# A second layer in another order of tokens, with half rounds in the value products

## The chip, the cores and the metric

The kernel runs on one core of a Trainium2 chip. The metric is the device time of one execution in microseconds (us), and lower is better.

## What is computed

Two layers of a small transformer on 256 tokens of width 2048, with 256 context tokens beside them, batch 1. The first layer is a Fourier mixer, the second an attention with 64 query heads of 64 columns on 8 key-value heads. Each layer ends in a projection (`w_out`) that is added to its input through a gate; the output is the normed `x`. What bears on the change is the attention:

```python
q, k, v, z = jnp.split(h @ w_in, [D_BRANCH, D_BRANCH + kvw, D_BRANCH + 2 * kvw], axis=-1)
kc, vc = jnp.split(hc @ w_in[:, D_BRANCH:D_BRANCH + 2 * kvw], 2, axis=-1)
q = _axial_rope(q...); k = _axial_rope(k...)
valid = abs(qpos - kpos) <= 128            # token against token; the context is seen by all
p = softmax(concat([where(mask, q @ keys * 64 ** -0.5, -1e30), sink]))[..., :-1]
y = (p @ vals) * silu(z)
x = x + gate * (y @ w_out)
return _rmsnorm(x, final_g)
```

A query in one half of the 256 tokens sees a key in the other half only if they are at most 128 apart. Counted in natural blocks of 32 tokens, a query block and a key block more than 4 blocks apart have no pair that the mask lets through.

## The kernel before

Everything is float32. Weights and activations are split into a high and a low part (`split`, `half_split`: a ScalarE cast and a VectorE difference), and a product is three matmuls (`mm3`, lines 79 to 81). Weights come in 1 MB loads on SP's queue (`raw`, L47).

**Order of tokens.** The host lays tokens out in an order of its own, `_perm`: tokens 0 to 128, then 255 down to 129. It suits the Fourier layer, and the kernel before keeps it to the end. The tiles have two blocks of 128 tokens, `tb` = 0 and 1, so that block 1 holds token 128 in its row 0 and then 255, 254 and so on. `rope` and `mask` (loaded by `cload`, L57, on POOL's queue, and followed there by `sink`) are tables in that order. The host puts the output back in order.

**Start of the second layer.** For each of 16 k-tiles, VectorE scales x (L931), ScalarE adds the shift and rounds to the high part `h` (L932), VectorE forms the low part (L933); s = 0 is the tokens, s = 1 the context. The k/v projection follows; `v` is copied out of PSUM by ScalarE (L959) and written to a DRAM tensor `vd` by POOL's queue (L961). `nsink` (L907) is a VectorE operation on `sink`. This part is ordered by the framework's planner, from its estimates of durations; the loop over heads is ordered by hand.

**The loop over heads.** 64 steps i, 8 for each key-value head: scores (`s_mm`), the mask and the maximum in one VectorE operation (L1215), exponentials and normalisation on ScalarE, and a VectorE transpose by blocks of 32 (`x_turn`, L1245) into `pall`, whose partitions are four groups g of 32 queries' blocks and whose columns are (head pair k, block of queries t, row i). Between them stand units of the projections (`emit_unit`). Queries are turned by `q_turn` (L1048).

**Value products.** After each 8 steps, `stage_o` (L1252), in two halves with a unit between, multiplies `vrep` and `pall`: for each key block b (16 of them: 4 + 4 blocks of tokens, 8 of context), each hh of 2 and each g of 4 one matmul of 32 rows by 64 columns with 256 moving columns. The 8 matmuls of one b lie in 8 different tiles of TensorE's array; all 16 b add up in PSUM. I call the 8 matmuls of one b a round. `emit_y` (L1261) multiplies the result by 0.5 and by z.

**The end.** `w_out` is applied to column blocks; `x2` holds the layer's input, loaded from the DRAM tensor `x1d` by POOL's queue (L1338). `finish(tb, ...)` takes the norm's root, scales four tiles of [128 tokens, 512 columns], in the order c = 2, 0, 3, 1, and stores each by one DMA to `out` (L1407): on SP's queue, and for tb = 1, c = 1 on ScalarE's. The stores of tb = 1 are the last thing that the kernel does.

Of the kernel before, what the change touches and what calls it, by code (L numbers as in the profile page):

```python
# [16 lines left out]
P = 128  # L17
# [12 lines left out]
def tile_dit(ctx: ExitStack, tc: tile.TileContext, a: dict, out: bass.AP):  # L30
# [24 lines left out]
    def cload(name, shape, q=None, pool=const):  # L55
        t = pool.tile(shape, F32, tag=name, name=name)
        (q or nc.gpsimd).dma_start(t, a[name])  # L57
        return t
# [841 lines left out]
    lay0.close()  # L900

    l1c = ctx.enter_context(tc.tile_pool(name="l1c", reuse_waits="tile", bufs=1))
    rope = cload("rope", [P, 2, 2, 64], pool=l1c)
    mask = cload("mask", [P, 2, 512], pool=l1c)
    sink = cload("sink", [P, 64], pool=l1c)
    nsink = l1c.tile([P, 64], F32, name="nsink")
    V.tensor_scalar(nsink, sink, -1.0, None, op0=ALU.mult)  # L907
# [12 lines left out]
    with tc.tile_pool(name="h1", reuse_waits="tile", bufs=16) as h1p:  # L920
        hx1 = []
        kT = []
        with tc.tile_pool(name="kvp", reuse_waits="tile", bufs=2) as kvp:
            hc1 = []
            for k in range(KT):
                hx = h1p.tile([P, 512], F32R, tag="h1", name="h1")
                hc = kvp.tile([P, 512], F32R, tag="h1c", name="h1c", bufs=16)
                t = kvp.tile([P, 512], F32, tag="ht", name="ht")
                for s, h in ((0, hx), (1, hc)):
                    q = slice(s * N, (s + 1) * N)  # L930
                    V.scalar_tensor_tensor(t[:, q], x1[k][:, q], gs1[:, k, s : s + 1], r_bc1[:, q] if k else rows1[s], op0=ALU.mult, op1=ALU.mult)  # L931
                    hx_act = S.activation(h[:, 0:N], t[:, q], AF.Identity, bias=sh1[:, k, s : s + 1]).ins  # L932
                    hx_end = V.scalar_tensor_tensor(h[:, N : 2 * N], t[:, q], sh1[:, k, s : s + 1], h[:, 0:N].bitcast(F32), op0=ALU.add, op1=ALU.subtract).ins  # L933
                if k == 0:
                    hx_first = (hx_end, hx_act)
                    with tc.issue_after(hx_act):
                        while turned:
                            x1_out(*turned.pop(0), kvp)
                hx1.append(hx)
                hc1.append(hc)  # L940
            o = [[psum() for _ in range(2)] for _ in range(4)]
            for kg in range(8):
                w = [(kv_h, kv_l)] if kg == 0 else ws_split(raw(a["wkv"][kg]))
                for j in range(2):
                    k = kg * 2 + j
                    if k == 1:
                        with tc.issue_after(hx_first[0]), tc.issue_after(hx_first[1]):
                            w.append(half_split(kv_raw, 1))
                    wh, wl = w[j]
                    for tb in range(4):  # L950
                        h = (hx1, hc1)[tb // 2][k]
                        c = (tb % 2) * P
                        for kv in range(2):
                            q = slice(kv * 512, (kv + 1) * 512)
                            mm3(o[tb][kv], h[:, c : c + P], h[:, N + c : N + c + P], wh[:, q], wl[:, q], k == 0, k == KT - 1)
            kr = []
            for tb in range(4):
                t = kvp.tile([P, 512], F32, tag="v", name="v", bufs=4)
                S.copy(t, o[tb][1])  # L959
                for g in range(4):  # L960
                    nc.gpsimd.dma_start(vd[:, :, tb * 4 + g, :].rearrange("h j d -> j h d"), t[g * 32 : g * 32 + 32].rearrange("p (h d) -> p h d", d=64))  # L961
                t = kvp.tile([P, 512], F32, tag="kr", name="kr", bufs=4)
                if tb < 2:
                    roped(t, o[tb][0], tb, kvp)
                else:
                    S.copy(t, o[tb][0])
                kr.append(t)
            for hp in range(4):
                o = psum()
                for tb in range(4):  # L970
                    PE.transpose(o[:, tb * P : (tb + 1) * P], kr[tb][:, hp * P : (hp + 1) * P], ident)
                t = act()
                S.copy(t, o)
                kT.append(t)
# [5 lines left out]
        with tc.tile_pool(name="ye", reuse_waits="tile", bufs=6) as yep, ExitStack() as ats:  # L980
# [62 lines left out]
            def q_turn(p2, qr):  # L1043
                o = psum()
                for pr in range(2):
                    for tb in range(2):
                        c = (p2 * 2 + pr) * P
                        PE.transpose(o[:, (pr * 2 + tb) * P : (pr * 2 + tb + 1) * P], qr[tb][:, c : c + P], ident)  # L1048
                return o

            def q_cast(hk, p2, o):
# [192 lines left out]
            def x_turn(i):  # L1244
                V.transpose(pall[:, i % 2, :, i // 2 % 4].rearrange("p b t i -> p t b i"), pts.pop(i).rearrange("p t (b j) -> p t b j", j=32))  # L1245

            def stage_o(oo, half):
                for b in range(half * 8, half * 8 + 8):
                    for hh in range(2):
                        for g in range(4):  # L1250
                            q = slice(g * 32, g * 32 + 32)
                            PE.matmul(oo[g][hh * 64 : hh * 64 + 64, 0:N], vrep[0][q, b, :], pall[q, hh, b].rearrange("p k t i -> p (k t i)"), start=b == 0, stop=b == 15)  # L1252

            def emit_y(hk, oo):
                th = szs.pop(hk)
                for p2 in range(2):
                    y1.append(act())
                    for g in range(4):
                        dst, z = (x.rearrange("p k (t g i) -> p k t g i", t=2, g=4)[:, :, :, g, :] for x in (y1[-1].rearrange("p (k n) -> p k n", k=2), th[:, p2 * 2 : p2 * 2 + 2]))
                        src = oo[g][:, p2 * P : (p2 + 1) * P].rearrange("p (k t i) -> p k t i", k=2, t=2)  # L1260
                        V.scalar_tensor_tensor(dst, src, 0.5, z, op0=ALU.mult, op1=ALU.mult)  # L1261

            for i in range(10):
                w_prep(pos[0])
# [65 lines left out]
            with tc.tile_pool(name="fin", reuse_waits="tile", bufs=1) as fp:  # L1330
# [4 lines left out]
                for tb in range(2):  # L1335
                    x2.append([act() for _ in range(4)])
                    for c in range(4):
                        nc.gpsimd.dma_start(x2[tb][c], x1d[tb, :, c * 512 : (c + 1) * 512])  # L1338
                fg = fp.tile([P, D], F32, name="fg")
                nc.gpsimd.dma_start(fg, a["fg"].broadcast_to([P, D]))  # L1340
                ss = fp.tile([P, P], F32, name="ss")
# [54 lines left out]
                def finish(tb, col, base):  # L1396
                    r, v, t = (fp.tile([P, 1], F32, name=f"f{n}{tb}") for n in "rvt")
                    root(r, v, t, ss[:, col : col + 1], base)
                    for c in (2, 0, 3, 1):
                        t = x2[tb][c]  # L1400
                        if c == 3:
                            V.scalar_tensor_tensor(t, t, r, fg[:, c * 512 : (c + 1) * 512], op0=ALU.mult, op1=ALU.mult)
                        elif c == 2:
                            V.tensor_scalar(t, t, r, None, op0=ALU.mult)
                        else:
                            S.activation(t, t, AF.Copy, scale=r)
                        (nc.scalar if tb and c == 1 else nc.sync).dma_start(out[tb * P : (tb + 1) * P, c * 512 : (c + 1) * 512], t)  # L1407

                held = []
                for kg in range(8):  # L1410
# [139 lines left out]
```

## Time and profile before

| | before |
|---|---|
| median of 3 runs | 1770.1 us (1769.8 to 1770.34) |
| profiled execution, device time | 1769.88 us |
| its span | 1768.1 us |
| TensorE (PE) busy | 1754.8 us, 99% |
| VectorE (DVE) busy | 1377.2 us, 78% |
| ScalarE (ACT) busy | 878.1 us, 50% |
| POOL busy | 184.5 us, 10% |
| value products, L1252 | 2048 records, 60.3 us, from 1190.8 to 1619.9 us |
| last stores, L1407 with tb = 1 | issued from 1762.6 us on |

The span runs from the first to the last instruction of the profiled execution; the device time has 1.8 us around it. PE is TensorE's matmuls, PEld its weight loads; SPq, ACTq and POOLq are the queues that issue DMAs. A row of a group reads: line, engine, operation, output and input by the program's names, shapes, count; then busy time in us and mean ns of one; then idle time just before it and what ended it. A row of the timeline reads: start and length in us, engine, line, operation, count, and in brackets the idle time before. A row of a line's instructions has durations as ns min/median/max, then first and last start. In the DMA view the first line is the mean busy share of the 16 DMA engines in 40 slices of the stretch, in tenths, and the second what they moved.

### The profile page before, as it was taken

To read this page: it belongs to the slowest core of one execution; us is meant where nothing else is said; L and a number is where in the kernel's file an instruction comes from. 1 tells how busy PE (TensorE), PEld (TensorE's weight loads), DVE (VectorE), ACT (ScalarE), POOL (GpSimd) and SP (SyncE) were. 2 spreads that over 40 slices of the span, in tenths; PEclk is the share of its full clock that TensorE was granted. 3 is DMA by queue.
4 is the path that set the end of the run, shared out by engine and by line. 5 is a ranking of instruction groups with operands and counts; after the bars stand their busy time and mean duration, and the time that the engine had idled before them with its cause. 6 is when DMAs were issued, how large, how long until landed. Compare 5 with 4: busy or idle time off the path is not lost.

```text
span 1768.1 us, 28034 instructions
## 1 busy us (share of the span) xinstructions
PE 1754.8 (99%) x10967; PEld 1480.5 (84%) x10967; DVE 1377.2 (78%) x2318; ACT 878.1 (50%) x1522; POOL 184.5 (10%) x223
## 2 busy tenths in 40 slices
PE   9999999999999999999999999999999999999998
PEld 7669999998888888888888888888888888887886
DVE  6769999978897887587986473798889888987455
ACT  6545444543222232333332352687778777876343
POOL 0001000020000010000000001133123302301000
PEclk9999999999999999999999999999999999999999
DMA  9994655476766777654566333544444444446553
GB/s 389 422 381 167 210 206 207 167 274 226 304 255 247 262 275 266 259 208 156 207 240 236 113 142 108 188 146 156 155 153 147 139 148 156 146 159 235 197 183 141
DMA packets 69108, 370.20 MB, mean 209 GB/s; under 512 B 8816, under 2 KB 11008, under 8 KB 35440
## 3 DMA queue, kind: packets, MB, share of 16 engines
q1 hardware_dynamic: 55600, 328.63, 50.5%
q0 software_dynamic: 9488, 32.95, 5.5%
q10 hardware_dynamic: 3888, 6.83, 1.1%
q8 instruction: 86, 1.41, 0.3%
q14 instruction: 46, 0.38, 0.1%
HBM read 353.16 MB, written 15.21 MB: 208 GB/s over the span
## 4 chain that ended last, share of the span: by engine, by line
PE 97%; ACT 1%; DVE 1%; DMA 0%; issue 0%; SPq 0%; DVEq 0%; ACTq 0%
PE ps L79 26%; PE ps L81 26%; PE ps L80 26%; PE ps L1177 7%; PE ps L1175 3%; PE ps L1252 3%; PE ps L347 2%; PE ps L1207 2%; PE ps L1206 2%; PE ps L1048 0%; DMA xn<-in_x 0%; PE ps L662 0%; PE ps L628 0%; PE ps L363 0%; DVE wl L1125 0%
## 5 line engine op out<-in xcount | busy, mean ns | idle before, releaser
L69 ACT CAST wh<-raw 128x1024 fp32r<-128x1024 f32 x178 | 186.9, 1053 | 402.9 <-PE ps L80 345.2
L70 DVE TENSOR_TENSOR wl<-raw,wh 128x1024 fp32r<-128x1024 f32 x178 | 219.8, 1235 | 137.9 <-ACT wh L69 137.8
L80 PE MATMUL ps<-hx,wh 128*128 128x512 f32 x700 | 272.6, 389 | 0.0
L79 PE MATMUL ps<-hx,wh 128*128 128x512 f32 x700 | 271.1, 390 | 0.0
L81 PE MATMUL ps<-hx,wl 128*128 128x512 f32 x700 | 271.1, 390 | 0.0
L1125 DVE TENSOR_TENSOR wl<-raw,wh 128x1024 fp32r<-128x1024 f32 x142 | 191.2, 1352 | 56.5 <-ACT wh L1119 56.0
L1119 ACT CAST wh<-raw 128x1024 fp32r<-128x1024 f32 x142 | 148.8, 1048 | 70.9 <-PE ps L80 58.2
L699 DVE CUSTOM_DVE_ANT_0 raw<-raw,cb 128x1024 f32<-128x1024 f32 x128 | 155.0, 1220 | 35.5 <-DMA raw<-in_adw 34.7
L79 PEld LDWEIGHTS ps<-hx,wh 128*128 128x128 f32 x700 | 131.4, 188 | 27.9 <-ACT hx L432 0.8
L81 PEld LDWEIGHTS ps<-hx,wl 128*128 128x128 f32 x700 | 131.5, 188 | 27.2
L80 PEld LDWEIGHTS ps<-hx,wh 128*128 128x128 f32 x700 | 131.5, 188 | 27.2
L699 DVE CUSTOM_DVE_ANT_0 junk<-raw,cb 128x1024 f32<-128x1024 f32 x96 | 117.2, 1221 | 27.4 <-DMA raw<-in_adw 14.1
L1177 PE MATMUL ps<-h,wh 128*128 128x512 f32 x512 | 127.3, 391 | 0.0
L79 PE MATMUL ps<-wh,h 128*128 128x512 f32 x320 | 124.9, 397 | 0.2 <-ACT h L932 0.2
L80 PE MATMUL ps<-wl,h 128*128 128x512 f32 x320 | 124.9, 390 | 0.0
L81 PE MATMUL ps<-wh,h 128*128 128x512 f32 x320 | 124.6, 391 | 0.0
L1224 ACT ACTIVATE p<-ps,mx 128x512 f32<-128x512 f32 x128 | 86.8, 683 | 52.9 <-DVE mx L1215 52.8
L1177 PEld LDWEIGHTS ps<-h,wh 128*128 128x128 f32 x512 | 94.2, 188 | 18.1
L1215 DVE CUSTOM_DVE_ANT_0 ps<-ps,mask,nsink 128x512 f32<-128x512 f32 x128 | 91.1, 752 | 0.5
L80 PE MATMUL ps<-act,wh 128*128 128x512 f32 x234 | 91.0, 389 | 0.0
L81 PE MATMUL ps<-act,wl 128*128 128x512 f32 x234 | 90.3, 390 | 0.3 <-DVE wl L70 0.3
L79 PE MATMUL ps<-act,wh 128*128 128x512 f32 x234 | 89.7, 389 | 0.0
(362 smaller groups left out, 3959.8 us busy)
## 6 DMA issues: line engine op xcount, KB each, us to landing
raw<-in_adw SPq DMA_DIRECT2D x64, 1024.0 KB, 4.9
raw<-in_wz SPq DMA_DIRECT2D x58, 1024.0 KB, 4.8
raw<-in_awp SPq DMA_DIRECT2D x32, 1024.0 KB, 12.4
raw<-in_wo SPq DMA_DIRECT2D x32, 1024.0 KB, 4.8
raw<-in_wq SPq DMA_DIRECT2D x32, 1024.0 KB, 4.7
raw<-in_wu SPq DMA_DIRECT2D x25, 1016.0 KB, 5.0
raw<-in_wo1b SPq DMA_DIRECT2D x16, 1024.0 KB, 4.8
act<-in_xT POOLq DMA_DIRECT2D x32, 256.0 KB, 5.6
```

What stands on the lines that cost most here:

```text
L69: cast[0] = S.copy(h, t[:, i * 1024 : (i + 1) * 1024]).ins
L70: V.tensor_tensor(l, t[:, i * 1024 : (i + 1) * 1024], h.bitcast(F32), op=ALU.subtract)
L79: PE.matmul(o, wh, xh, start=start, stop=False)
L80: PE.matmul(o, wh, xl, start=False, stop=False)
L81: return PE.matmul(o, wl, xh, start=False, stop=stop).ins
L699: V.tensor_tensor_reduce(junk if s == 0 and i < 3 else wf, wf, cb[:, s], 1.0, 0.0, ALU.mult, ALU.add, acc[:, i, kh, fg * 2 + f, s : s + 1])
L1119: cast[0] = S.copy(h, t[:, i * 1024 : (i + 1) * 1024]).ins
L1125: V.tensor_tensor(ready[n][1], ready[n][2], ready[n][0].bitcast(F32), op=ALU.subtract)
L1175: PE.matmul(o[0][:, 0:N], wl[:, q], hx1[k][:, 0:N], start=False, stop=False)
L1177: PE.matmul(o[0], wh[:, q], hx1[k], start=k == 0, stop=k == KT - 1)
L1215: V.tensor_tensor_reduce(so[tb], so[tb], mask[:, tb, :], -0.125, nsink[:, i : i + 1], ALU.add, ALU.min, mx[:, tb : tb + 1])
L1224: S.activation(pt[:, tb, :], so[tb], AF.Exp, bias=mx[:, tb : tb + 1], scale=-1.0, accum_out=sm[:, tb : tb + 1])
```

## The change

From the second layer on, tokens stand in another order: block 0 as before, block 1 turned by one, so that it holds 255 down to 128. Every block of 32 rows is then a natural block of 32 tokens, in block 1 the other way round. For this

- `rope` and `mask` are loaded in pieces from the same tables: 3 and 10 DMAs instead of 1 and 1, all on POOL's queue;
- `ht` gets 640 columns; for s = 0 a VectorE copy of one column puts token 128 behind the others, and L932 and L933 read two runs of 128 columns with a gap;
- `q_turn` writes the four blocks of 32 of tb = 1 in reverse, so that group g, t = 1 is natural query block 4 + g;
- the x2 tiles of tb = 1 are loaded by two DMAs each, of 127 rows and of 1 row, and the output of tb = 1 is stored by two DMAs each, of 127 rows and of 1 row.

In the value products each g then has 3 key blocks of 16 in which one of its two query blocks t lies more than 4 blocks away. For these only the columns of the other t are multiplied, 128 instead of 256. `rounds(g)` puts them at positions 3, 6 and 11 of the 16 for every g, so that all 8 matmuls of a round have the same number of columns. The factor 0.5 of `emit_y` moves to the copy of v.

```diff
@@ -900,8 +900,16 @@
     lay0.close()
 
     l1c = ctx.enter_context(tc.tile_pool(name="l1c", reuse_waits="tile", bufs=1))
-    rope = cload("rope", [P, 2, 2, 64], pool=l1c)
-    mask = cload("mask", [P, 2, 512], pool=l1c)
+    rope = l1c.tile([P, 2, 2, 64], F32, name="rope")
+    nc.gpsimd.dma_start(rope[:, :, 0], a["rope"][:, :, 0])
+    nc.gpsimd.dma_start(rope[0:127, :, 1], a["rope"][1:128, :, 1])
+    nc.gpsimd.dma_start(rope[127:128, :, 1], a["rope"][0:1, :, 1])
+    mask = l1c.tile([P, 2, 512], F32, name="mask")
+    for c0, c1, s0 in ((0, 128, 0), (128, 255, 129), (255, 256, 128), (256, 512, 256)):
+        nc.gpsimd.dma_start(mask[:, 0, c0:c1], a["mask"][:, 0, s0 : s0 + c1 - c0])
+    nc.gpsimd.dma_start(mask[:, 1, 128:512], a["mask"][:, 1, 128:512])
+    for r0, r1, s0 in ((0, 31, 97), (31, 32, 0), (32, 64, 65), (64, 96, 33), (96, 128, 1)):
+        nc.gpsimd.dma_start(mask[r0:r1, 1, 0:128], a["mask"][s0 : s0 + r1 - r0, 1, 0:128])
     sink = cload("sink", [P, 64], pool=l1c)
     nsink = l1c.tile([P, 64], F32, name="nsink")
     V.tensor_scalar(nsink, sink, -1.0, None, op0=ALU.mult)
@@ -925,12 +933,18 @@
             for k in range(KT):
                 hx = h1p.tile([P, 512], F32R, tag="h1", name="h1")
                 hc = kvp.tile([P, 512], F32R, tag="h1c", name="h1c", bufs=16)
-                t = kvp.tile([P, 512], F32, tag="ht", name="ht")
+                t = kvp.tile([P, 640], F32, tag="ht", name="ht")
                 for s, h in ((0, hx), (1, hc)):
                     q = slice(s * N, (s + 1) * N)
-                    V.scalar_tensor_tensor(t[:, q], x1[k][:, q], gs1[:, k, s : s + 1], r_bc1[:, q] if k else rows1[s], op0=ALU.mult, op1=ALU.mult)
-                    hx_act = S.activation(h[:, 0:N], t[:, q], AF.Identity, bias=sh1[:, k, s : s + 1]).ins
-                    hx_end = V.scalar_tensor_tensor(h[:, N : 2 * N], t[:, q], sh1[:, k, s : s + 1], h[:, 0:N].bitcast(F32), op0=ALU.add, op1=ALU.subtract).ins
+                    u = t[:, 258:514] if s else t[:, 0:258].rearrange("p (b i) -> p b i", b=2)[:, :, 0:128]
+                    rb = r_bc1[:, q] if k else rows1[s]
+                    V.scalar_tensor_tensor(t[:, s * 258 : s * 258 + N], x1[k][:, q], gs1[:, k, s : s + 1], rb, op0=ALU.mult, op1=ALU.mult)
+                    hh, hl = h[:, 0:N], h[:, N : 2 * N]
+                    if s == 0:
+                        V.tensor_copy(t[:, 256:257], t[:, 128:129])
+                        hh, hl = (x.rearrange("p (b i) -> p b i", b=2) for x in (hh, hl))
+                    hx_act = S.activation(hh, u, AF.Identity, bias=sh1[:, k, s : s + 1]).ins
+                    hx_end = V.scalar_tensor_tensor(hl, u, sh1[:, k, s : s + 1], hh.bitcast(F32), op0=ALU.add, op1=ALU.subtract).ins
                 if k == 0:
                     hx_first = (hx_end, hx_act)
                     with tc.issue_after(hx_act):
@@ -956,7 +970,7 @@
             kr = []
             for tb in range(4):
                 t = kvp.tile([P, 512], F32, tag="v", name="v", bufs=4)
-                S.copy(t, o[tb][1])
+                S.activation(t, o[tb][1], AF.Copy, scale=0.5)
                 for g in range(4):
                     nc.gpsimd.dma_start(vd[:, :, tb * 4 + g, :].rearrange("h j d -> j h d"), t[g * 32 : g * 32 + 32].rearrange("p (h d) -> p h d", d=64))
                 t = kvp.tile([P, 512], F32, tag="kr", name="kr", bufs=4)
@@ -1045,7 +1059,10 @@
                 for pr in range(2):
                     for tb in range(2):
                         c = (p2 * 2 + pr) * P
-                        PE.transpose(o[:, (pr * 2 + tb) * P : (pr * 2 + tb + 1) * P], qr[tb][:, c : c + P], ident)
+                        dst = o[:, (pr * 2 + tb) * P : (pr * 2 + tb + 1) * P]
+                        if tb:
+                            dst = dst.rearrange("p (b i) -> p b i", b=4)[:, ::-1]
+                        PE.transpose(dst, qr[tb][:, c : c + P], ident)
                 return o
 
             def q_cast(hk, p2, o):
@@ -1244,21 +1261,35 @@
             def x_turn(i):
                 V.transpose(pall[:, i % 2, :, i // 2 % 4].rearrange("p b t i -> p t b i"), pts.pop(i).rearrange("p t (b j) -> p t b j", j=32))
 
+            def rounds(g):
+                empty = lambda b, n: b < 8 and abs((b if b < 4 else 11 - b) - n) > 4
+                one = [(b, 1 - t) for t in range(2) for b in range(8) if empty(b, 4 * t + g)]
+                both = [(b, None) for b in range(16) if b not in dict(one)]
+                return both[0:3] + one[0:1] + both[3:5] + one[1:2] + both[5:9] + one[2:3] + both[9:13]
+
+            value = [rounds(g) for g in range(4)]
+
             def stage_o(oo, half):
-                for b in range(half * 8, half * 8 + 8):
+                for n in range(half * 8, half * 8 + 8):
                     for hh in range(2):
                         for g in range(4):
                             q = slice(g * 32, g * 32 + 32)
-                            PE.matmul(oo[g][hh * 64 : hh * 64 + 64, 0:N], vrep[0][q, b, :], pall[q, hh, b].rearrange("p k t i -> p (k t i)"), start=b == 0, stop=b == 15)
+                            b, t = value[g][n]
+                            o, p = oo[g][hh * 64 : hh * 64 + 64, 0:N], pall[q, hh, b]
+                            if t is None:
+                                p = p.rearrange("p k t i -> p (k t i)")
+                            else:
+                                o, p = o.rearrange("p (k t i) -> p k t i", k=4, t=2)[:, :, t], p[:, :, t]
+                            PE.matmul(o, vrep[0][q, b, :], p, start=n == 0, stop=n == 15)
 
             def emit_y(hk, oo):
                 th = szs.pop(hk)
                 for p2 in range(2):
                     y1.append(act())
                     for g in range(4):
-                        dst, z = (x.rearrange("p k (t g i) -> p k t g i", t=2, g=4)[:, :, :, g, :] for x in (y1[-1].rearrange("p (k n) -> p k n", k=2), th[:, p2 * 2 : p2 * 2 + 2]))
+                        dst, z = (x.rearrange("p k (b i) -> p k b i", b=8)[:, :, g : 8 - g : 7 - 2 * g] for x in (y1[-1].rearrange("p (k n) -> p k n", k=2), th[:, p2 * 2 : p2 * 2 + 2]))
                         src = oo[g][:, p2 * P : (p2 + 1) * P].rearrange("p (k t i) -> p k t i", k=2, t=2)
-                        V.scalar_tensor_tensor(dst, src, 0.5, z, op0=ALU.mult, op1=ALU.mult)
+                        V.tensor_tensor(dst, src, z, op=ALU.mult)
 
             for i in range(10):
                 w_prep(pos[0])
@@ -1335,7 +1366,8 @@
                 for tb in range(2):
                     x2.append([act() for _ in range(4)])
                     for c in range(4):
-                        nc.gpsimd.dma_start(x2[tb][c], x1d[tb, :, c * 512 : (c + 1) * 512])
+                        for r0, r1, s0 in ((0, 127, 1), (127, 128, 0)) if tb else ((0, P, 0),):
+                            nc.gpsimd.dma_start(x2[tb][c][r0:r1], x1d[tb, s0 : s0 + r1 - r0, c * 512 : (c + 1) * 512])
                 fg = fp.tile([P, D], F32, name="fg")
                 nc.gpsimd.dma_start(fg, a["fg"].broadcast_to([P, D]))
                 ss = fp.tile([P, P], F32, name="ss")
@@ -1404,7 +1436,12 @@
                             V.tensor_scalar(t, t, r, None, op0=ALU.mult)
                         else:
                             S.activation(t, t, AF.Copy, scale=r)
-                        (nc.scalar if tb and c == 1 else nc.sync).dma_start(out[tb * P : (tb + 1) * P, c * 512 : (c + 1) * 512], t)
+                        q, (e0, e1) = slice(c * 512, (c + 1) * 512), (nc.scalar, nc.sync) if c == 1 else (nc.sync, nc.sync)
+                        if tb:
+                            e0.dma_start(out[P + 1 : 2 * P, q], t[0:127])
+                            e1.dma_start(out[P : P + 1, q], t[127:128])
+                        else:
+                            nc.sync.dma_start(out[0:P, q], t)
 
                 held = []
                 for kg in range(8):
```

## The prediction

> **What bounds the kernel now.** I read the page's busy table and chain first, then the waits of TensorE, the busy times by stretch, and the groups of the lines that the diff touches, shapes kept apart.
>
> ```profile
> PE 1754.8 (99%) x10967; PEld 1480.5 (84%) x10967; DVE 1377.2 (78%) x2318; ACT 878.1 (50%) x1522; POOL 184.5 (10%) x223
> ...
> PE 97%; ACT 1%; DVE 1%; DMA 0%; issue 0%; SPq 0%; DVEq 0%; ACTq 0%
> ```
> ```profile
> PE ps L313 <- POOL ident masks.py:199: 1.9, 1, 1.9
> ...
> PE ps L79 <- ACT h L932: 0.2, 1, 0.2
> ```
> ```profile
> 1245.00:1300.00 55.00, 55.00 (x498) 46.00 (x498) 46.93 (x87) 41.51 (x81) 16.16 (x14) 1.00 0.44 149
> ```
> ```profile
> L1175 PE MATMUL ps<-h,wl 128*128 128x256 f32 x512 | 68.1, 284 | 0.0
> ...
> L1252 PE MATMUL ps<-pall,vr 32*64 32x256 f32 x2048 | 60.3, 378 | 0.4 <-issue 0.4
> ...
> L1206 PE MATMUL ps<-kkh,qb 128*128 128x512 f32 x64 | 24.9, 390 | 0.0
> ```
>
> TensorE is the chain: 97% of it, and its wait list holds single waits of under 2 us. In the attention stage (the row from 1245 to 1300: us, PE, PEld, DVE, ACT, POOL) it is busy for all 55 us at full clock, VectorE for 46.9. So a microsecond of matmul taken out there is a microsecond of the end, as long as VectorE, with 8 us free in 55, keeps up. The value products are the group of L1252, 60.3 us in all. After the last matmul there is a tail that no matmul hides:
>
> ```profile
> 1759.14 0.28 PE L81 MATMUL ps<-wh,ys 128*128 128x256 f32 x1
> ...
> 1762.61 1.30 SPq L1407 DMA_DIRECT2D out<-act  x3
> 1763.38 0.38 ACTq L1407 DMA_DIRECT2D out<-act  x1
> ```
>
> The four stores of the second token block are issued from 1762.61 on, and the span ends at 1768.1. Everything that they get longer is added to the time in full.
>
> **The value products.** There are 8 key-value heads, 16 rounds each, and a round is 2 x 4 small products, each of which the trace shows as two records (2048 for 1024 products). Eight records run side by side, so the 2048 records are 256 passes, 60.3 / 256 = 0.2355 us each, edges included. The change gives 128 instead of 256 columns to 3 rounds of 16: 3 x 2 x 8 = 48 passes. The price of a column: 512 against 256 columns is (390 - 284) / 256 = 0.414 ns in the rows of L1206 and L1175, which need one record per product. The f32 pass shows 0.2355 / 256 = 0.92 ns, edges included, about twice that. So a half pass is 128 x 2 x 0.414 = 0.106 us shorter, and 48 of them 5.1 us. Bounds: half of the whole pass, 48 x 0.118 = 5.7 us, and nothing, if records cannot follow each other more closely than now (60.3 / 2048 = 29 ns on average; no row shows a closer mean). I take 5.1, since columns explain most of the pass.
>
> [...]
>
> **Same work in other words.** emit_y uses a plain product instead of a scaled one; the two forms cost alike:
>
> ```profile
> L1191 DVE SCALAR_TENSOR_TENSOR th<-th,zs 128x256 f32<-128x256 f32 x32 | 13.3, 417 | 0.0
> L1189 DVE TENSOR_TENSOR zs<-ps,zs 128x256 f32<-128x256 f32 x32 | 13.3, 414 | 0.0
> ```
>
> The factor 0.5 goes into the four ScalarE copies of v, the reversed blocks into the addresses of the 32 transposes with tb = 1, no instruction more: 0, hidden by ScalarE, which is idle half of the span; uncovered it would be some 0.1 us a copy.
>
> **The start of the second layer.** Each of 16 k gets a copy of one column on VectorE between the scaling (L931) and ScalarE's L932.
>
> ```profile
> 1010.62 0.54 POOL L57 DMA_DIRECT2D sink<-in_sink  x1
> ...
> 1011.06 0.17 DVE L91 RECIPROCAL qr<-qt 128x4 f32<-128x4 f32 x1
> ...
> 1013.60 0.91 ACT L932 ACTIVATE h<-ht,sh 128x256 fp32r<-128x256 f32 x2
> ...
> 1014.16 0.50 PE L79 MATMUL ps<-wh,h 128*128 128x512 f32 x1 [0.20 <-ACT h L932]
> ...
> 1016.44 0.20 DVE L907 TENSOR_SCALAR nsink<-sink 128x64 f32<-128x64 f32 x1 [0.50 <-DMA sink<-in_sink]
> ...
> 1019.35 0.48 DVE L933 SCALAR_TENSOR_TENSOR h<-ht,sh,h 128x256 fp32r<-128x256 f32 x1
> ...
> 1019.74 1.07 PE L79 MATMUL ps<-wh,h 128*128 128x512 f32 x4
> ```
>
> A tiny VectorE operation takes 0.17 us (L91). Only the first k is waited for (0.20 us), and the second comes just in time (1019.35 against 1019.74): +0.3 us, bounds 0 and 16 x 0.17 = 2.7.
>
> On POOL's queue rope and mask go from 2 issues to 13, all ahead of sink: 11 x 0.54 = 5.9 us. rope and mask are first used at 1096.8 and 1136.3, long after; the cover is the whole k/v projection. But nsink (L907) sits in VectorE's queue and already waits 0.5 us for sink, and behind it queue the h tiles that TensorE needs by 1019.74. Kept at its place it would hold VectorE, and soon TensorE, for up to 5.9 us. The planner orders this part by its own estimate of when a load lands, and before it came within 0.5 us, so I take 0 and keep 5.9 as a bound. In the last part x2's second block takes 4 more POOL issues, for tiles first used after 1630.7 (L1344 starts its chain); the issues ran from 1566.7 to 1610.9, so 0 (4 x 0.54 = 2.1 us without those 20 us of cover).
>
> ```profile
> L912 DVE TENSOR_TENSOR kr<-ps,rope x2: 685/688/692, 1096.8 to 1099.2; 128x512 f32<-128x512 f32 x2
> ...
> L1215 DVE CUSTOM_DVE_ANT_0 ps<-ps,mask,nsink x128: 745/752/759, 1136.3 to 1603.8; 128x512 f32<-128x512 f32 x128
> ...
> L1338 POOL DMA_DIRECT2D act<-x1d x8: 536/536/595, 1566.7 to 1610.9; - x8
> ...
> L1344 DVE TENSOR_TENSOR ps<-ps,gbc x10: 432/689/700, 1630.7 to 1759.5; 128x512 f32<-128x512 f32 x8, 128x256 f32<-128x256 f32 x2
> ```
>
> **The last stores.** Each of the four becomes a store of 127 rows and one of 1 row, on the queues of SP and ACT. Four more issues at some 0.43 us (1.30 / 3) are the small part. The large part is how 127 rows are dealt to the 16 DMA engines. The first block's four stores, in a stretch of 6 us:
>
> ```profile
> GB/s 0 0 0 0 0 0 0 0 0 0 0 0 96 410 423 410 369 396 410 328 382 369 314 287 355 328 410 369 355 341 300 219 82 41 0 0 0 0 0 0
> DMA packets 576, 1.05 MB, mean 175 GB/s; under 512 B 64, under 2 KB 64, under 8 KB 576
> ...
> q1 hardware_dynamic: 576, 1.05, 50.5%
> ```
>
> A store of 128 rows is 144 packets: 128 rows of 2 KB and 16 tiny ones (64 for four stores), one for each engine. So each engine gets 128 / 16 = 8 rows, an equal share. For 127, a prime, no equal share exists on more than one engine. The bounds lie far apart: 8 rows on one engine as now, or all 127. A row takes one engine between 77 ns (16 x 2048 B at the peak of 423 GB/s) and 94 ns (50.5% of 16 x 6 us over 512 rows). The rate of the middle is 85 ns. Even shares: the tail gains only issues, at most 4 x 0.43 = 1.7 us, of which I let half, 0.8, stick out past the first stores' transfer. All on one: 4 x 127 x 85 ns = 43.2 us instead of 32 rows on each engine x 94 ns = 3.0 us, that is +40.2 (77 ns: +36.1; 94 ns: +44.8). The four cannot run beside each other if they use the same engine. The nearest row, with its equal shares, speaks for a division without remainder, so I take one engine.
>
> [...]
>
> **Sum.** The profiled execution took 1769.9 us, its span 1768.1 and 1.8 around it, 0.2 under the median of the runs, 1770.1. 1769.9 - 5.1 + 0.3 + 40.2 = 1805.3 us.
>
> **Rivals.** (a) The stores spread evenly, so the tail stays: 1769.9 - 5.1 + 0.3 + 0.8 = 1765.9, faster. It decides where a 127-row store needs under some 1.9 us (0.7 us now, plus 4.8 / 4 each). For it speaks that every store in the trace spreads over 16 engines; against it the equal shares. (b) One engine, but the half rounds save nothing, because issue, not columns, sets the pace: 1805.3 + 5.1 = 1810.4. For it: 29 ns a record is short. Against: the column price explains the pass. [...] (c) One engine, and nsink holds VectorE: 1805.3 + 5.9 = 1811.2.
>
> **Chances.** The forecast 0.62, (b) 0.13, (c) 0.12, (a) 0.10, something else 0.03. One engine is thus likely at 0.87, and (b) and (c) only add to it. The range holds these three: from 77 ns a row (1801.2), less the 0.6 us more that the products could save and a little, 1799, to 1815, (b) or (c) with some 4 us for slower rows. A change of 0.2%, 3.5 us, is about what can be told from none: (a) is 4 us below, so of its 0.10 some 0.06 count as faster and 0.04 as same; slower 0.90.
>
> **What would show it.** Right: the group of L1252 falls from 60.3 to about 55 us, its half records 0.1 us shorter; the DMA line after the last matmul shows a busy share of one in 16 for some 40 us at about 25 GB/s; landing of the last stores of tens of us. Wrong: that line full again for 3 us; L1252's busy time unchanged (b); a DVE row of L907 with several us of idle time from sink, and PE waits on h (c).

## The result and the profile after

The changed kernel takes 1812.12 us (median of 5 runs, 1811.99 to 1813.54) against 1770.01 us: a ratio of 1.0241 (1.0226 to 1.0256), 42.1 us slower. The profiled execution took 1813.16 us with a span of 1811.0, so it stands 43.3 us above the profiled one of before, 1769.88. TensorE is busy for less time than before (1752.2 against 1754.8 us) in a longer span. The chain that ended last no longer holds it for 97%:

```profile
PE 1752.2 (97%) x10967; PEld 1479.2 (82%) x10967; DVE 1378.3 (76%) x2334; ACT 878.7 (49%) x1522; POOL 195.6 (11%) x238
...
PE 40%; ACT 0%; DVE 0%; issue 0%
```

The shares of that chain no longer add up to 100%: followed back from the late stores it loses its thread, so I do not read times from it. I set the starts of the same records of both traces against each other instead. That gives the account of the 43.3 us:

| stretch | after minus before, us |
|---|---|
| first layer | +0.2 |
| start of the second layer, the wait for `h` and what follows it | +6.5 |
| attention and the output projection, to the last matmul and the first last store | -3.2 |
| from the first store of tb = 1 (1766.19 against 1762.61) to the end of the span | +39.3 |
| around the span (2.2 against 1.8) | +0.4 |
| sum | +43.2 |

**The end.** The timeline of the changed kernel from its first late store on (start, length, queue, line):

```profile
1766.19 0.29 SPq L1441 DMA_DIRECT2D out<-act  x1
1766.52 0.50 SPq L1442 DMA_DIRECT2D out<-act  x1
1766.96 0.50 ACTq L1441 DMA_DIRECT2D out<-act  x1
1767.13 5.54 SPq L1441 DMA_DIRECT2D out<-act  x1
1772.77 18.16 SPq L1442 DMA_DIRECT2D out<-act  x1
1791.03 0.23 SPq L1441 DMA_DIRECT2D out<-act  x1
1791.35 10.01 SPq L1442 DMA_DIRECT2D out<-act  x2
```

And its DMA view from 1766 to 1811 us, in 40 slices:

```profile
GB/s 4 7 18 25 25 22 25 25 25 25 25 25 25 25 25 25 25 25 25 25 25 25 25 25 25 27 25 25 25 25 25 25 25 25 25 25 25 25 13 0
DMA packets 520, 1.05 MB, mean 23 GB/s; under 512 B 8, under 2 KB 8, under 8 KB 520
```

The busy times of a stretch inside it (us, PE, PEld, DVE, ACT, POOL, granted clock, DMA share, GB/s):

```profile
1770.00:1790.00 20.00, 0.00 (x0) 0.00 (x0) 0.00 (x0) 0.00 (x0) 0.00 (x0) 0.50 0.07 25
```

The rate stands at 25 GB/s for 40 us, where whole stores move some 400 (their row is shown with the first experiment); the DMA share of 0.07 is about one engine in 16. The tiny packets tell the same: 8, one for each of the eight stores, where the four stores of 128 rows had 64. The issues on SP show something more. Single issues take 5.5, 18.2 and (two together) 10.0 us: SP itself is held in them while the stores move at 25 GB/s. Nothing else is left for it to do here, and the rate stands throughout, so I count no cost for it beyond the transfers.

**The value products.** The group, without and with the shapes apart:

```profile
L1283 PE MATMUL ps<-pall,vr 32*64 32x256 f32 (+1 forms) x2048 | 56.2, 359 | 1.5 <-issue 1.5
```
```profile
L1283 PE MATMUL ps<-pall,vr 32*64 32x256 f32 x1664 | 56.0, 380 | 1.5 <-issue 1.5
...
L1283 PE MATMUL ps<-pall,vr 32*64 32x128 f32 x384 | 12.0, 269 | 0.0
```

60.3 us became 56.2. A half record is 380 - 269 = 111 ns shorter. (The busy times of the two shapes overlap in time, so they do not add up.)

**The start of the second layer.** This is the part that I had not foreseen. The waits of TensorE, its longest first:

```profile
PE ps L79 <- ACT h L946: 4.7, 1, 4.7
PE ps L313 <- POOL ident masks.py:199: 1.9, 1, 1.9
PE ps L1283 <- issue: 1.5, 1, 1.5
```

In place of a wait of 0.2 us for `h` stands one of 4.7. The timeline shows what ScalarE did before it made `h`, L946 being the line that was L932:

```profile
1013.70 0.48 DVE L941 SCALAR_TENSOR_TENSOR ht<-act,gs 128x256 f32<-128x256 f32 x1
...
1014.60 0.51 ACT L946 ACTIVATE h1c<-ht,sh 128x256 fp32r<-128x256 f32 x1 [0.89 <-DVE ht L941]
...
1014.88 0.21 DVE L944 COPY ht<-ht 128x1 f32<-128x1 f32 x2
1015.01 1.05 ACT L855 COPY xo<-ps 128x512 f32<-128x512 f32 x2
...
1016.91 1.07 ACT L69 CAST wh<-raw 128x1024 fp32r<-128x1024 f32 x1
...
1017.86 0.54 ACT L946 ACTIVATE h1c<-ht,sh 128x256 fp32r<-128x256 f32 x1
...
1018.27 0.92 ACT L946 ACTIVATE h<-ht,sh 128x256 fp32r<-128x256 f32 x2
...
1018.84 0.79 PE L79 MATMUL ps<-wh,h 128*128 128x512 f32 x1 [4.67 <-ACT h L946]
```

The column copy itself takes 0.1 us (L944, two in 0.21), and it is done at 1015.1. But on VectorE the scalings of k = 0 and 1 stand ahead of it, four of 0.48 us from 1013.30 on, and ScalarE, whose order the planner sets too, makes the context's `h1c` first, then four copies of `xo`, a cast and the next `h1c`, and only at 1018.27 the `h` that TensorE has waited for since 1014.17. Before, `h` came first of all. Nothing in those 3 us needed to be ahead of it, as the kernel with a tied order shows below; the planner, which orders this part, put it there once `h` had one operation more in front of it.

The wait then costs more than its length. The busy times of the changed kernel by stretch, with columns as above:

```profile
1012.00:1014.00 2.00, 1.83 (x16) 1.79 (x16) 0.73 (x3) 0.87 (x3) 2.00 (x1) 1.00 0.78 293
1014.00:1018.00 4.00, 0.17 (x2) 0.00 (x0) 1.57 (x6) 3.40 (x7) 3.91 (x8) 0.81 0.47 22
1018.00:1020.00 2.00, 1.16 (x3) 0.97 (x4) 1.98 (x4) 2.00 (x4) 0.19 (x1) 0.50 0.90 269
1020.00:1022.00 2.00, 2.00 (x7) 1.52 (x6) 2.00 (x5) 0.70 (x2) 2.00 (x5) 0.50 1.06 366
1022.00:1024.00 2.00, 2.00 (x8) 1.58 (x7) 1.94 (x7) 0.81 (x2) 0.37 (x1) 0.68 1.10 257
1024.00:1028.00 4.00, 4.00 (x19) 3.33 (x18) 3.69 (x9) 2.76 (x6) 0.00 (x0) 1.00 0.58 229
```

During the wait the granted clock falls to 0.50, and it is back at 1.00 only after some 4 us of work: 7 and 8 matmul records in 2 us instead of 10 or 11. The means of the rows, 0.81 and 0.68, put the fall at about 1016.5, 2.3 us into the wait, and the return at about 1023.3. Some 4.4 us of work at half speed lose about 2 us, and 4.5 us of longer wait with these 2 make the 6.5 us of the account. What sets the moments of the fall and of the return these rows do not show.

`nsink` (now L915), which the prediction's third rival had hold VectorE, was simply moved behind by the planner, and waits hardly more or less than before:

```profile
1021.80 0.57 POOL L57 DMA_DIRECT2D sink<-in_sink  x1
...
1028.55 0.20 DVE L915 TENSOR_SCALAR nsink<-sink 128x64 f32<-128x64 f32 x1 [0.34 <-DMA sink<-in_sink]
```

### The profile page after: what moved, and what is told of

Read it like the earlier page. It is cut to its first block, busy times and chain, and to the rows that moved or that the text cites. A ratio compares the mean times of both kernels' runs of the same rounds, so it can differ in the third digit from the quotient of the medians.

```text
span 1811.0 us, 28079 instructions
## 1 busy us (share of the span) xinstructions
PE 1752.2 (97%) x10967; PEld 1479.2 (82%) x10967; DVE 1378.3 (76%) x2334; ACT 878.7 (49%) x1522; POOL 195.6 (11%) x238
## 5 line engine op out<-in xcount | busy, mean ns | idle before, releaser
L1194 PEld LDWEIGHTS ps<-h,wh 128*128 128x128 f32 x512 | 94.1, 188 | 18.2
```

What stands on the lines that cost most here:

```text
L1194: PE.matmul(o[0], wh[:, q], hx1[k], start=k == 0, stop=k == KT - 1)
```

## The experiments

The kernel before, run beside them on the same chips, took 1769.8 to 1769.9 us (medians).

**Whole last stores.** The changed kernel with one store of 128 rows for each tile of tb = 1; the host turns the rows.

```
-  e0.dma_start(out[P + 1 : 2 * P, q], t[0:127])
-  e1.dma_start(out[P : P + 1, q], t[127:128])
+  e0.dma_start(out[P : 2 * P, q], t)
```

> The changed kernel, but each of the four stores of tb = 1 is again one DMA of 128 rows, in the order of the tile; the host puts the rows back. Theory A (a store of 127 rows runs on one DMA engine): from the first of these stores to the end of the span it takes 5.5 us as before the change, not 44.8, so the time falls by 39.3 us to about 1772.8 (1772 to 1774). Theory B (the tail is long for another reason, such as the ScalarE and VectorE steps before the stores): the time stays above 1790. Either way the wait at the start of the second layer (4.7 us) stays.

Measured: 1773.30 us (1772.32 to 1773.96), ratio to before 1.0019 (1.0010 to 1.0029). So 38.8 us of the 42.1 are the division into 127 + 1, and the rest of the change does not make up for itself: it costs 3.5 us (1.8 to 5.1). The same end in this kernel's DMA view, 1762 to 1771.2 us:

```profile
GB/s 18 0 0 0 0 0 0 0 0 0 0 0 0 0 0 0 0 0 0 98 419 401 410 347 374 401 267 329 374 374 338 267 143 18 0 0 0 0 0 0
```

**126, 113 and 127 rows.** Is it the number, or that the tile is cut at all? The 127 rows are cut again, into 126 + 1 and into 113 + 14, so both have more stores than the changed kernel, 12 instead of 8.

```
-  e0.dma_start(out[P + 1 : 2 * P, q], t[0:127])
+  e0.dma_start(out[P + 1 : P + 127, q], t[0:126])       # 113: out[P + 1 : P + 114], t[0:113]
+  e0.dma_start(out[P + 127 : 2 * P, q], t[126:127])     # 113: out[P + 114 : 2 * P], t[113:127]
```

> The changed kernel with each store of 127 rows cut into 126 rows and 1 row, so that there are twelve stores in the end instead of eight, and nothing else differs. Theory A (the rows are dealt out in equal shares; 126 = 14 x 9 fits 14 engines): the tail is short again, about 1774 (1772.5 to 1777, four more issues of 0.4 us). Theory B (the number of stores, or the single rows, make the tail long): it stays at 1812 or goes up, since there are more of both.

> The changed kernel with each store of 127 rows cut into 113 rows, again a prime, and 14 rows. Theory A (equal shares, so 113 rows on one engine at 26 GB/s, 79 ns a row): 4 x 14 = 56 rows fewer on that engine, less 4 x 1 that come back with the 14 rows on 14 engines: the tail falls by 52 x 0.079 = 4.1 us, to about 1808 (1806 to 1810). Theory B (rows are dealt out unevenly, with a remainder, so that 113 spreads like 112): about 1774. Theory C (127 is slow because it is odd or because it is close to 128): near 1774 or 1812.

Measured (one run each): 126 rows 1775.54 us, 113 rows 1808.83 us. One row less, and 36.6 us are gone, with four stores more. The DMA views of the ends, first 126 rows (1764 to 1773.4 us), then 113 (1762 to 1806.7 us):

```profile
GB/s 0 0 0 0 0 0 0 0 0 0 0 0 0 0 166 296 296 270 218 192 270 296 270 227 235 279 261 262 288 244 209 157 18 0 9 0 0 0 0 0
DMA packets 576, 1.05 MB, mean 112 GB/s; under 512 B 64, under 2 KB 64, under 8 KB 576
```
```profile
GB/s 130 0 0 0 7 13 18 50 24 26 26 26 27 46 26 26 26 26 50 26 26 26 26 26 26 26 26 26 26 26 24 50 26 26 26 26 26 26 15 0
```

126 rows move at some 260 GB/s, 113 rows at 26, with short peaks of about 50 where the 14-row stores run beside them. 126 is 14 x 9; 113 and 127 are primes. That cutting as such is slow is out; the number of rows decides, and equal shares, from which the prediction argued, are borne out by 128, 126 and two primes. The tiny packets show the share of 126 rows too: of the 64 in the row above, eight belong to the eight stores of one row, one each as in the changed kernel, and 56 are left for the four stores of 126 rows, 14 each. So, counted by their tiny packets, 128 rows went out as 16 shares of 8 and 126 as 14 shares of 9, and 127 rows as one, at 25 GB/s and a DMA share of 0.07; 113 rows at 26 GB/s fit one share as well. No odd number of rows that is not a prime was tried, so these runs do not tell whether it is enough to be odd.

**The same stores on POOL's queue.** All eight late stores of the changed kernel are issued by POOL.

```
-  e0.dma_start(out[P + 1 : 2 * P, q], t[0:127])
-  e1.dma_start(out[P : P + 1, q], t[127:128])
+  nc.gpsimd.dma_start(out[P + 1 : 2 * P, q], t[0:127])
+  nc.gpsimd.dma_start(out[P : P + 1, q], t[127:128])
```

> The changed kernel (1812.1 us) with the eight last stores, 127 rows and 1 row each as they are, issued on POOL's queue instead of SP's and ScalarE's. Theory A (one engine for 127 rows is a matter of the queues of SP and ScalarE; on POOL's the 127-row loads of x2 landed after 5.3 us, too soon for one engine): the tail is short, 1774 to 1778. Theory B (127 rows run on one engine on any queue): 1810 to 1814.

Measured (one run): 1778.50 us, just over the upper end that was expected. The DMA view from 1760 to 1776.4 us:

```profile
DMA  9930000000000007957868788620000000000000
GB/s 385 360 140 0 0 0 0 0 0 0 0 0 0 0 0 180 220 236 184 260 228 222 220 259 251 202 98 0 0 0 0 0 0 0 0 0 0 0 0 0
...
out<-act POOLq DMA_DIRECT2D x4, 254.0 KB, 3.1
```

The same 127 rows that take SP's and ScalarE's queues 10 us each land in 3.1 us from POOL's, at some 220 GB/s. So the price is one of the queue and the number together. The rate is nearly nine times the 25 GB/s, and the busy share of the 16 engines stands at 5 to 9 tenths in these slices (0.07 in the changed kernel), so many of them take part; how many the view does not count. This kernel is 5.2 us slower than the one with whole stores, though its first store is issued earlier (1765.1 against 1765.7). Its eight issues, 0.5 us each, and the lower rate let the last bytes move at about 1771 instead of 1770 us. The larger part comes behind them: from there to the end of the span pass some 5.3 us, against 1.4 with whole stores. What fills them the runs do not show.

**The order at the second layer's start.** The kernel with whole stores, in which VectorE's and ScalarE's first operations are tied: for k = 0 and 1 the other scalings come after the first column copy, and the other activations after the first `h`.

```
+  with tc.issue_after(cp[0]) if cp and k < 2 else nullcontext():
       V.scalar_tensor_tensor(t[:, s * 258 : s * 258 + N], ...)
-  V.tensor_copy(t[:, 256:257], t[:, 128:129])
+  cp.append(V.tensor_copy(t[:, 256:257], t[:, 128:129]).ins)
+  with tc.issue_after(acts[0]) if acts and k < 2 else nullcontext():
       hx_act = S.activation(hh, u, AF.Identity, ...)
+  acts.append(hx_act)
```

> The kernel with whole stores (run beside this one), with the planner told to put the column copy of the first k right behind its scaling on VectorE, and the first h ahead of everything else on ScalarE. Theory A (the column copy let the planner put h behind four ScalarE copies and a cast, and TensorE waits for h 4.7 us, and then runs at half clock): most of the 6.5 us that the second layer starts late comes back, so about 1767 (1766 to 1769), 3 us under the kernel before. Theory B (the eleven more POOL loads hold back the sink load, and so VectorE): they are all still there, so the time stays near 1772.8.

Measured: 1766.48 us (1765.90 to 1767.53), ratio 0.9982 (0.9972 to 0.9991). That is 6.8 us less than with the planner's order, and faster than both kernels of this case. The timeline:

```profile
1013.86 0.15 DVE L945 COPY ht<-ht 128x1 f32<-128x1 f32 x1
...
1014.05 0.51 ACT L948 ACTIVATE h<-ht,sh 128x256 fp32r<-128x256 f32 x1 [0.28 <-DVE ht L945]
...
1014.61 0.50 PE L79 MATMUL ps<-wh,h 128*128 128x512 f32 x1 [0.38 <-ACT h L948]
```

Copy and wait are there as predicted (0.15 us and 0.38 instead of 0.20), and all 13 pieces of `rope` and `mask` still stand ahead of `sink`.

**Without the copy.** The whole-store kernel without L944; ScalarE reads columns 0 to 255.

```
-  u = t[:, 258:514] if s else t[:, 0:258].rearrange("p (b i) -> p b i", b=2)[:, :, 0:128]
+  u = t[:, 258:514] if s else t[:, 0:256].rearrange("p (b i) -> p b i", b=2)
-  V.tensor_copy(t[:, 256:257], t[:, 128:129])
```

> The kernel with whole stores (1773.3 us), without the copy of one column in the 16 scalings (so h is not turned by one, and the rest takes it as if it were). The thirteen POOL loads of rope and mask stay. Theory A (the copy alone let the planner move h behind the ScalarE copies): the wait of 4.7 us goes, about 1766.5, as with the pinned order. Theory B (the POOL loads do it): 1773.3.

Measured: 1766.07 us (ratio 0.9978, 0.9968 to 0.9987), and the wait is back at 0.2 us, by itself:

```profile
PE ps L79 <- ACT h L945: 0.2, 1, 0.2
```

So the one extra operation in front of `h` changed the planner's order, and not the pieces of the tables, which this kernel still loads.

**Tables in one piece.** The kernel with the tied order, with `rope` and `mask` laid out by the host and loaded by one DMA each (13 issues become 2).

```
-  rope = l1c.tile([P, 2, 2, 64], F32, name="rope")
-  ...
+  rope = cload("rope", [P, 2, 2, 64], pool=l1c)
+  mask = cload("mask", [P, 2, 512], pool=l1c)
```

> The kernel with the pinned start (1766.5 us), with rope and mask laid out by the host in the new order and loaded by one DMA each, as before the change. Theory A (eleven POOL loads more are hidden): 1766.5, within 1 us. Theory B (they cost what they take on POOL, 5.9 us, or collide with the loads of weights at the start of the second layer): 1761 to 1765.

Measured: 1766.50 us (ratio 0.9981, 0.9971 to 0.9990) against 1766.48 us. The pieces cost nothing.

**What the half rounds are worth.** The whole-store kernel with all 16 rounds at 256 columns, and the kernel before, in its own order of tokens, with three rounds of 16 at 128 columns.

```
+  one = [(b, None) for b, _ in one]                     # in rounds(g): no half round
```
```
+  if b in (3, 6, 11):                                   # in the kernel before
+      o, p = o.rearrange("p (k t i) -> p k t i", k=4, t=2)[:, :, 0], p[:, :, 0]
```

> The kernel with whole stores (1773.3 us), with all sixteen rounds of the value products at 256 columns again, in the new order of tokens. Theory A (a half pass saves 107 ns, but the records behind it then come one by one every 17 ns, which costs some 0.1 to 0.2 us a half): 3.2 to 4.1 us slower, 1776.5 to 1777.4. Theory B (columns alone count): 5.1 us slower, 1778.4. Theory C (the half rounds are worth nothing, and the 3 us by which the offset shrinks over the attention come from the new order): 1773.3.

> The kernel before, with nothing changed but that rounds 3, 6 and 11 multiply only the first query block's 128 columns (it leaves out products that the old order needs). Theory A (the half rounds save the same without the new order, the 3.4 us by which whole stores beat the run with full rounds): 1766.4 (1765.5 to 1767.2). Rival (the saving shows only together with the new order, whose queries or v copies are cheaper): 1769.9.

Measured: without half rounds 1776.72 us (ratio 1.0039, 1.0024 to 1.0054), so the half rounds are worth 3.4 us; in the kernel before they are worth 4.0 us (1765.85; 0.9978, 0.9968 to 0.9988). Both lie under the 5.1 of the column price, and nearer to it than to nothing; but their intervals are some 2 to 3 us wide to each side and do not exclude 5.1. The starts of the same records, from the first value products to the last matmul, are closer: against the kernel before this part is 4.1 us shorter with whole stores, 0.2 longer without half rounds, and 4.1 shorter in the kernel before with half rounds, so 4.3 and 4.1. (The total says 3.4 in part because the second layer's start costs 7.0 us in the profile of the whole-store kernel and 6.5 in that without half rounds, for the same wait.) The group without half rounds:

```profile
L1284 PE MATMUL ps<-pall,vr 32*64 32x256 f32 x2048 | 60.2, 377 | 0.7 <-issue 0.7
```

60.2 against 56.1 us in the whole-store kernel: 4.1, not 5.1. The starts of the records say where the rest stays. A stage is 8 rounds, 16 passes. In one tile, full passes start 216 ns apart and half passes 109, so each half pass gives up its 107 ns:

| stage of 8 rounds, first to last record, us (first and last head aside) | half passes | kernel before | by columns | kernel after |
|---|---|---|---|---|
| first half (positions 3 and 6) | 4 | 3.33 to 3.44 | 2.90 to 3.01 | 2.99 to 3.06 |
| second half (position 11) | 2 | 3.33 | 3.12 | 3.20 |

In the second halves of the kernel before, the 8 records of a pass start 7 ns apart. In the changed kernel they start some 17 ns apart from the half passes on, to the end of the stage, so its last tile ends some 0.07 us later than columns allow. First halves are less regular: four of the six in the table start their records 18 to 22 ns apart in the kernel before already, and those are the ones of some 3.43 us; in the changed kernel they end with 19 to 29 ns. 16 stages x 0.07 us are 1.1 us, about what lies between 5.1 and 4.1. Why the starts keep that distance the records do not say.

**All rounds half, and half rounds early.** Whether a floor in the pace of issue eats the columns: the whole-store kernel with 15 rounds of 16 at 128 columns, and the tied kernel with the three half rounds at positions 1, 2 and 9.

```
   b, t = value[g][n]
+  t = None if n == 0 else t or 0
```
```
-  return both[0:3] + one[0:1] + both[3:5] + one[1:2] + both[5:9] + one[2:3] + both[9:13]
+  return both[0:1] + one[0:2] + both[1:7] + one[2:3] + both[7:13]
```

> The kernel with whole stores (1773.3 us), with every round but the first of each head at 128 columns (it leaves out most of the second query block's value products). That is 12 more half rounds for each of 8 heads, 192 half passes more. Theory A (records come no faster than one in 17 ns for long, so that a half pass of eight takes 136 ns): 192 x 0.080 - 48 x 0.02 = 14.3 us faster, about 1759 (1757 to 1760). Theory B (columns alone: 109 ns): 192 x 0.107 = 20.5 us faster, 1752.8. A half of eight half rounds would last 2.2 us by A and 1.9 by B.

> The kernel with the pinned start (1766.5 us), with the half rounds at positions 1, 2 and 9 of the 16 instead of 3, 6 and 11. In the trace of the pinned kernel a first half of the value products lasts 2.99 to 3.06 us and a second 3.20, where columns alone would make 2.91 and 3.12: after a half pass the records of a pass start 17 ns apart instead of 7, so the last tile ends late. Theory A (the spread comes once TensorE's queue has been drained by two half passes on end, wherever they stand): the same 2.99 to 3.06 and 3.20. Theory B (the queue is fullest at the start of a half, so that early half rounds are fed in time): 2.91 and 3.12, 1.1 us less in all, 1765.4.

Measured (one run each): 1758.35 us and 1766.78 us. The first total falls almost on the figure that a pace of 17 ns a record gives, and yet that theory falls. In the second halves of the third to the seventh head, 16 half passes in a row, the passes of the first tile start 109 ns apart as columns have it, and the 128 records take 1.83 us, some 14 ns each: under 17. What keeps the total from the full price is another thing, the waits of TensorE for issue (its list of waits, and the group):

```profile
PE ps L1284 <- issue: 4.0, 4, 2.4
```
```profile
L1284 PE MATMUL ps<-pall,vr 32*64 32x128 f32 (+1 forms) x2048 | 36.8, 280 | 4.0 <-issue 4.0
```

The group's busy time falls by 56.1 - 36.8 = 19.3 us, the kernel by 15.0; 3.3 of the 4.3 between are longer waits for issue (4.0 against 0.7). 2.4 of the 4.0 stand in the last head, whose two halves follow each other without a projection between them, the others in the first two heads. Early half rounds change nothing (3.20 and 2.99 to 3.05 us a stage), so their place is not what costs.

## Why the prediction was right, and where it was not

**The last stores: right.** Predicted +40.2 us from 4 x 127 rows x 85 ns on one engine; measured +39.3, and at 25 GB/s a row of 2 KB takes 82 ns. (The sum took 85 ns a row on one engine beside 94 ns on sixteen; with 85 for both it is +40.5, which changes nothing.) Three runs stand behind the cause: whole stores take back 38.8 us, 126 rows nearly as much, 113 rows 3.3 us, near the 4.1 that one engine with 14 rows fewer a store gives. Rival (a), an even spread, is out for these queues. On POOL's the same rows moved at some 220 GB/s and landed in 3.1 us, which the choice between "one engine" and "equal shares" in the prediction did not consider. That the four stores would share the same engine was the author's assumption, for which no row of before stands; the 25 GB/s and the share of 0.07 through 40 us show it.

**The value products: mechanism right, size off.** The term was 5.1 us; the group fell by 4.1, and the two kernels that isolate it differ by 3.4 and 4.0 us. The price of a column held (a half pass is 107 ns shorter, predicted 106), so rival (b) is out. Its 29 ns a record is no limit either: with half passes in a row the records came some 14 ns apart (128 in 1.83 us). Missing in the sum were the stagger of the records after a half pass, about 1.1 us, and the wait for issue in the last head, which is 0.4 us in the kernel before, 1.5 in the changed kernel's profile, and 0.6 to 1.4 in the other runs with three half rounds.

**The start of the second layer: the step that failed.** Predicted +0.3 us (bounds 0 to 2.7), measured +6.5. The sum priced the copy as an instruction on VectorE, and that was right to a tenth (0.1 to 0.2 us). It took the order around it as given. That part is ordered by the planner, as the prediction itself said of `nsink` a paragraph later, and one operation more in front of `h` was enough for ScalarE to take 3 us of other work first. The bound was too narrow for the same reason: 16 copies are not the most that such an edit can cost. Here it cost a wait of 4.7 us, and the clock at 0.50 took about 2 us more.

**Tables and x2 in pieces: 0, right.** The tables by the pair 1766.50 and 1766.48 us; for x2 no run was made, but in the trace the lines that use its tiles (L1376, L1377) wait for TensorE and never for a load. The copies of v with the factor 0.5, for which the prediction named some 0.1 us each without a row, took 600 ns instead of 587 (L973 and L959). Rival (c) did not happen: L915 waited 0.34 us. Only half of its sign was seen, the wait of TensorE on `h`, and that had another cause. Its figure of 1811.2 lies close to the result by chance, since another wait of about the size took its place. That is worth noting: the total would have supported the wrong rival.

**The sum.** 1805.3 lies 6.8 us under the median, 7.9 under the profiled execution: 6.2 from the start of the second layer, 1.9 from the attention (3.2 instead of 5.1), 0.4 around the span, 0.2 in the first layer, less 0.9 of the tail makes 7.8. That the result still lies in the range is in part luck: its upper end was set for rivals (b) and (c), neither of which happened, and it took in a wait that no term or rival named.

## What to carry to other kernels

Where a tile is cut for the sake of one row, look at the number of rows that is left and at the queue that moves it, above all at the end of a kernel, where nothing covers a transfer: on SP's and ScalarE's queues 127 rows were 16 times slower than 128 (25 GB/s against some 400), and 126 were not (some 260). In a part that a planner orders, an added operation has two prices, its own time and the order that comes of it; look in the trace after for an engine that does unrelated work while the critical one waits, and tie the first operations down, which here turned a loss of 3.5 us (with whole stores) into a gain of 3.3. A total that lands on a rival's figure does not show the rival: twice here (1811.2, and the pace of 17 ns) the trace showed another cause of the same size.

## What the runs showed of the hardware

- The queue decides with the number of rows: 254 KB in 127 rows took about 10 us from SP's and ScalarE's queues (at 25 GB/s) and landed in 3.1 us from POOL's. A load of the same 127 rows for x2 on POOL's queue landed in 5.3 us, too soon for one engine at 25 GB/s; that of 127 rows of `rope`, two runs to a row, took 9.0 us where 128 rows took 3.5, which was not followed up.
- SP was held in issuing, up to 18.2 us at a time, while the stores of 127 rows moved at 25 GB/s. Nothing else was queued behind them here, so no run shows what that does to a later load.
- Matmuls of 32 x 64 in eight tiles with 128 columns came a record every 14 ns through 16 passes (128 records in 1.83 us). What sets their starts 17 ns apart after half passes, and what the waits for issue of up to 2.4 us are in the kernel with 15 half rounds of 16, stays open.
